# Six of ten token tiles transposed by VectorE in 32-blocks and put in place through DRAM, in place of TensorE's transposes

## The chip, the cores and the metric

One core of a Trainium2 chip runs the whole kernel. The core has a matrix engine (TensorE, PE in the profile), a vector engine (VectorE, DVE), a scalar engine (ScalarE, ACT), GpSimd (POOL) and SyncE (SP), whose queue issues nearly all DMAs here; 16 DMA engines carry them out. The metric is device time in microseconds, the median of a few runs. Lower is better.

## The reference

One encoder layer (depth 1, so the convolution mixer and no mLSTM) on 1024 prompt tokens and 256 sample tokens, model width 1024, in float32:

```python
h = rms_norm(x, norms[i, 0])
mix = short_conv_mixer(h, conv_w_in[j], conv_w[j], conv_w_out[j])
x = x + rms_norm(mix, norms[i, 1])
h = rms_norm(x, norms[i, 2])
x = x + rms_norm(swiglu(h, ffn_w_in[i], ffn_w_out[i]), norms[i, 3])
```

`short_conv_mixer` is a product to three times the width, a gated convolution over three tokens, and a product back to the width (`conv_w_out`); `swiglu` is a product to 2 x 2816 columns, `silu(gate) * up`, and a product back.

## The kernel before

Every float32 product is done as three products of high and low parts (`TERMS`), and the products over prompt tokens by a Strassen scheme over quarters of the operands (a11, a12, a21, a22 and their sums s1 to s4). The 1280 tokens are ten tiles of 128 (`i` = 0 to 9; 8 and 9 are the sample tokens). The stages, in order:

1. The first product and the convolution, features on partitions. The gated result, in high and low parts, goes to DRAM as `zd`.
2. The second product, `mm2`, one token tile at a time in the order 0, 4, 1, 5, 2, 6, 3, 7, 8, 9 (`ORDER2`), tokens on partitions. `load_z` brings a tile's operand from `zd` to `zs`; `mm2(i)` makes 48 products of 512 columns into two PSUM banks `mx`. Then `after_mm2(i)` runs six steps: ScalarE squares `mx` (sums `n1`), a factor is made by VectorE and GpSimd, VectorE makes `x1` = scaled `mx` plus the input tile `xt` and SP stores it to DRAM (`x1d`), ScalarE squares `x1` (sums `n2`), another factor, and VectorE writes the normalised tile `ht`.
3. The FFN needs the tokens on the free axis. `transposes(i)` turns `ht` in eight 128x128 pieces on TensorE into two PSUM banks `tr`; ScalarE and VectorE copy them into the quarters `ar` (`ar[0, 0]` is a11, `ar[1, 1]` is a22; the second index is the half of the tokens). In stage 2 the transposes of a tile stand inside the `mm2` of the tile two places later.
4. The FFN's two products, and the last norm.

`early_sums` splits the high and low parts of a slice of a11 and makes the slice's Strassen sums in place, as soon as the two token tiles of that slice are in `ar`. The first FFN weights `F0` are loaded and split in the same stretch (`wgf0`, `wuf0`, then at `n == 6` `wt24f0`, `wt13f0`). The last of these take buffer places that `zs` of a finished tile leaves (`wt13f0` takes that of `zs6`).

What sets the order: stage 2 is left to a scheduler, which writes one instruction list for each engine; an engine runs its list strictly in order, and so does SP with its DMAs. The entry to the FFN (`entry`, with tiles 8 and 9) is written out by hand. Buffers are places that are handed on: `get` takes the place longest free, `put` gives one back, and whoever takes a place waits for all that still use it. The kind "a" has three places, for `xt` and `x1`, kind "s" two, for `ht`. PSUM banks are taken in turn, eight of them (`new_ps`), but in `entry` by fixed numbers: the product of tile 8 in 4 and 5, that of 9 in 2 and 3, the transposes of tile 3 in 6 and 7, those of tile 7 in 0 and 1.

Of the kernel before, what the change touches and what calls it, by code (L numbers as in the profile page):

```python
# [8 lines left out]
F32 = mybir.dt.float32  # L9
# [5 lines left out]
P = 128  # L15
D = 1024
KD = D // P
# [19 lines left out]
def encoder_kernel(ctx: ExitStack, tc: tile.TileContext, xT, x, g0T, gB, cwT, w1, w2, w3, w4, out_p, out_s):  # L37
    nc = tc.nc
# [6 lines left out]
    dram = ctx.enter_context(tc.tile_pool(name="dram", bufs=1, space=bass.MemoryType.DRAM))  # L45
# [12 lines left out]
    def get(name, shape, dt=F32, kind="b"):  # L58
        if kind == "as":
            kind = "s" if free["s"] else "a"  # L60
        tag = free[kind].pop(0)
        t = mem.tile([P, *shape], dt, tag=tag, name=name)
        held[id(t)] = (t, tag)
        return t

    def put(*tiles):
        for t in tiles:
            tag = held.pop(id(t))[1]
            free[tag[0]].append(tag)
# [13 lines left out]


    zd = dram.tile([2, len(UNITS), P, 2, KD, P], F32, tag="zd", name="zd")
    x1d = dram.tile([NT, P, D], F32, tag="x1d", name="x1d")
    actd = dram.tile([len(UNITS), KP, P, 14 * P], F32, tag="actd", name="actd")

# [16 lines left out]
    def copy(out, a):  # L105
        nc.scalar.activation(out, a, AF.Copy)  # L106
# [3 lines left out]
    def new_ps(name, bank=None):  # L110

        if bank is None:
            bank = turn[0] % 8
            turn[0] += 1
        return ps.tile([P, 512], F32, tag=f"bank{bank}", name=name)
# [55 lines left out]
    def load(u, left=True, right=True):  # L171
        if u is None:
            return
        if u not in raw:
            raw[u] = get(f"wr{uname(u)}_", [4, 512])
        if u[0] == "p":
            tiles = [w1[u[1] * KD + 2 * u[2] + h] for h in (0, 1)]
        else:
            tiles = [w3[h * KF + u[1]] for h in (0, 1)]
        tiles = [t.rearrange("p (b c) -> p b c", b=2) for t in tiles]  # L180
        if left:
            nc.sync.dma_start(raw[u][:, 0:4:3], tiles[0])
        if right:
            nc.sync.dma_start(raw[u][:, 1:3], tiles[1])

    def make(u, what):

        if u is None:
            return
        rw = raw[u]  # L190
        if what == "sums":
            sub(rw[:, 0], rw[:, 1], rw[:, 0])
            sub(rw[:, 1], rw[:, 2], rw[:, 1])
            sub(rw[:, 2], rw[:, 0], rw[:, 2])
            add(rw[:, 3], rw[:, 3], rw[:, 2])
            return
        blocks = {"g": slice(0, 4, 3), "u": slice(1, 3), "t13": slice(0, 2), "t24": slice(2, 4)}[what]
        t = wb[what, u] = get(f"w{what}{uname(u)}_", [2, 2, 512], F32R)
        split(t[:, 0], t[:, 1], rw[:, blocks])
        sums_made[u] = sums_made.get(u, 0) + what.startswith("t")  # L200
        if sums_made[u] == 2:
            put(raw.pop(u))
# [577 lines left out]
    def load_z(i, k0=0, k1=KD):  # L780
        if i not in zs:
            zs[i] = get(f"zs{i}", [2, KD, P], F32R)
        src = zd[i // 4, i % 4] if i < 8 else zd[i - 8, 4]
        nc.sync.dma_start(f32(zs[i][:, :, k0:k1]), src[:, :, k0:k1])

    ORDER2 = [i for uu in UNITS for i in uu]
# [30 lines left out]
    ar = {(kh, c): get(f"ar{kh}{c}", [KH, 512]) for kh in (0, 1) for c in (0, 1)}  # L817
    hts, mx = {}, {}

    def transposes(i, banks=(None, None)):  # L820
        for q in range(2):
            o = new_ps(f"tr{i}_{q}", banks[q])
            for k in range(4):
                nc.tensor.transpose(
                    o[:, k * P : (k + 1) * P], hts[i][:, (4 * q + k) * P : (4 * q + k + 1) * P], ident
                )
            ov = o.rearrange("p (k t) -> p k t", k=4)
            if i < 8:
                t0 = i % 4 * P
                dst = ar[q, i // 4][:, :, t0 : t0 + P]  # L830
                if q:
                    nc.vector.tensor_copy(dst, ov)
                else:
                    copy(dst, ov)
            else:
                t0 = (i - 8) * P
                copy(hs[0][:, 4 * q : 4 * q + 4, t0 : t0 + P], ov)
                left.append((i, q, ov))
        put(hts.pop(i))

    left = []

    def take_left():
# [6 lines left out]
    def mm2(*tiles, ks=range(KD)):  # L850
        for i in tiles:
            if i not in mx:
                mx[i] = [new_ps(f"mx{i}_{h}", MX_BANKS.get((i, h))) for h in range(2)]
        for k in ks:
            for i in tiles:
                for j, (w, part) in enumerate(TERMS):
                    for h in range(2):
                        nc.tensor.matmul(  # L858
                            mx[i][h], zs[i][:, part, k], w2t[k][:, w, h * H : (h + 1) * H],
                            start=k == 0 and j == 0, stop=k == KD - 1 and j == 2,  # L860
                        )
# [38 lines left out]
    def after_mm2(i):  # L900
        for step in (norm_squares, norm_factor, norm_residual, norm_squares2, norm_factor2, norm_end):
            step(i)
# [3 lines left out]
    def load_xt(i):  # L906
        xts[i] = get(f"xt{i}", [D], kind="a")
        nc.sync.dma_start(xts[i], x[i])
# [4 lines left out]
    def early_sums(t):  # L913

        a, b, d = (q[:, :, t] for q in (a11, a21, a22))
        split(*(q[:, :, t] for q in cb["a11"]), a)
        add(b, b, d)
        sub(a, a, b)
        add(s3[:, :, t], d, a)
# [6 lines left out]
    for n, i in enumerate(ORDER2[:8]):  # L926
        if n == 0:
            mm2(i, ORDER2[1])
        elif n > 1:
            early = KD - 2 if n < 4 else 4  # L930
            mm2(i, ks=range(early))
            transposes(ORDER2[n - 2])
            mm2(i, ks=range(early, KD))
            if n == 4:
                cb["a11"] = [get(f"a11{p}", [KH, 512], F32R) for p in "hl"]
                s3 = get("s3", [KH, 512])
                early_sums(slice(0, P))
            if n == 6:
                early_sums(slice(P, 2 * P))
        after_mm2(i)  # L940
        if n:
            load_z(ORDER2[n + 1])
            load_xt(ORDER2[n + 1])
        if n == 4:
            load(F0)
            for what in ("g", "u", "sums"):
                make(F0, what)
        if n == 6:
            for what in ("t24", "t13"):
                make(F0, what)  # L950
# [691 lines left out]
```

## Time and profile before

| | |
|---|---|
| median of 3 runs | 1252.47 us (1251.35 to 1254.31) |
| the profiled execution | 1250.58 us |
| its span, first to last instruction | 1248.7 us |
| granted TensorE clock, mean | 0.998 |
| TensorE busy | 1236.0 us (99%) |
| VectorE / ScalarE / GpSimd busy | 835.0 / 463.9 / 25.6 us |
| DMA | 207.37 MB, 166 GB/s on average |

A row of a timeline reads: start, length (both us), engine, line, operation, out<-in, shapes, how many, and in brackets how long the engine stood idle before it and what ended that. SPq is SP's queue issuing a DMA. A row of the chain reads: start, length, engine, tile and line, how many. A row of waits reads: who waited for whom, total us, times, longest. A row of windows reads: the stretch, its length, busy time and instructions of PE, weight loads, VectorE, ScalarE and GpSimd, the granted clock, the share of the DMA engines, GB/s. A row of DMA issues reads: out<-in, queue, how many, KB each, median us from issue to landing; of DMA queues: packets, MB, the share of 16 engines' time. Numbers in names are left out there, so `tr`, `ar`, `zs` stand for all tiles; stage 2 runs from about 311 to 429 us.

### The profile page before, as it was taken

The numbers are of one execution on the slowest core, as the hardware profiler recorded it, in microseconds if no ns is written. First come the engines' busy times: TensorE is split into PE (matmuls) and PEld (weight loads), VectorE is DVE, ScalarE is ACT, GpSimd is POOL, SyncE is SP. The second block draws the span as 40 slices with busy tenths as digits, with TensorE's granted clock in tenths as the row PEclk, the third lists the DMA queues.
The fourth block names the chain that finished last, engine by engine and source line by source line (L and its number), as shares of the span: only waits on it lengthen the run. The fifth ranks groups of instructions, "written<-read, shape, count | busy, mean of one in ns | idle before, by whom it ended". The sixth has DMA issues, their size and how long they took to land.

```text
span 1248.7 us, 15941 instructions
## 1 busy us (share of the span) xinstructions
PE 1236.0 (99%) x6239; PEld 1052.2 (84%) x6239; DVE 835.0 (67%) x1157; ACT 463.9 (37%) x695; POOL 25.6 (2%) x49
## 2 busy tenths in 40 slices
PE   9999999999999999999999999999999999999997
PEld 7888888888888888888888888888888888888886
DVE  6986856657376787475466564755657479869566
ACT  8643333234233554343343343443434342102011
POOL 0000000000010100000000000000000000000000
PEclk9999999999999999999999999999999999999999
DMA  8323041416854215254262452542626798766894
GB/s 307 123 85 110 34 152 35 118 51 221 303 184 168 85 61 172 89 178 127 92 194 88 150 160 89 182 129 87 194 95 205 259 315 303 275 209 220 287 329 178
DMA packets 186123, 207.37 MB, mean 166 GB/s; under 512 B 8000, under 2 KB 146368, under 8 KB 185024
## 3 DMA queue, kind: packets, MB, share of 16 engines
q1 hardware_dynamic: 185616, 205.83, 49.1%
q8 instruction: 49, 0.80, 0.3%
q10 hardware_dynamic: 432, 0.53, 0.1%
q14 instruction: 26, 0.21, 0.1%
HBM read 134.89 MB, written 71.43 MB: 165 GB/s over the span
## 4 chain that ended last, share of the span: by engine, by line
PE 91%; DMA 3%; DVE 3%; ACT 2%; issue 1%; SPq 0%; POOL 0%; POOLq 0%; DVEq 0%; ACTq 0%
PE xo L1441 12%; PE mx L858 6%; PE zo L1441 6%; PE yo L1441 3%; DMA wrf__3033<-w 1%; PE xp__1068 L213 1%; PE xf__3503 L213 1%; PE xp__901 L213 1%; PE xf__7645 L213 1%; PE xf__7466 L213 1%; PE xf__7253 L213 1%; PE xf__7079 L213 1%; PE xf__6866 L213 1%; PE xf__6692 L213 1%; PE xf__6479 L213 1%; PE xf__6305 L213 1%
## 5 line engine op out<-in xcount | busy, mean ns | idle before, releaser
L858 PE MATMUL mx<-w2s,zs 128*128 128x512 f32 x480 | 111.1, 391 | 0.0
L858 PEld LDWEIGHTS mx<-w2s,zs 128*128 128x128 f32 x480 | 89.5, 188 | 18.3
L106 ACT ACTIVATE st<-act 128x640 fp32r<-128x640 f32 x77 | 56.8, 737 | 93.8 <-DMA actd<-st 62.9
L97 DVE TENSOR_TENSOR st<-act,st 128x640 fp32r<-128x640 f32 x77 | 63.2, 821 | 21.4 <-ACT st L106 20.9
L100 DVE TENSOR_TENSOR y<-y,xo 128x512 f32<-128x512 f32 x85 | 58.2, 685 | 27.4 <-PE xo L1441 27.1
L1441 PE MATMUL xo<-w4t,us 128*128 128x512 f32 x273 | 68.9, 389 | 0.0
L1441 PEld LDWEIGHTS xo<-w4t,us 128*128 128x128 f32 x273 | 51.2, 188 | 10.7
L1441 PE MATMUL xo<-w4t,ut 128*128 128x512 f32 x222 | 55.5, 389 | 0.0
L106 ACT ACTIVATE w4t<-w4r 128x1024 fp32r<-128x1024 f32 (+1 forms) x23 | 23.5, 1023 | 72.1 <-DVE w4r L97 58.4
L1441 PEld LDWEIGHTS xo<-w4t,ut 128*128 128x128 f32 x222 | 41.7, 188 | 8.7
L100 DVE TENSOR_TENSOR y<-y,zo 128x512 f32<-128x512 f32 x45 | 30.8, 685 | 17.3 <-PE zo L1441 17.0
L1441 PE MATMUL xo<-w4b,ut 128*128 128x512 f32 x165 | 41.6, 390 | 0.0
L1441 PE MATMUL zo<-w4t,ut 128*128 128x512 f32 x165 | 41.5, 389 | 0.0
L1441 PE MATMUL zo<-w4b,ut 128*128 128x512 f32 x165 | 41.5, 389 | 0.0
L1473 ACT ACTIVATE junk<-y 128x1024 f32<-128x1024 f32 (+1 forms) x12 | 11.0, 919 | 73.7 <-DVE y L100 72.4
L1441 PEld LDWEIGHTS xo<-w4b,ut 128*128 128x128 f32 x165 | 31.0, 188 | 6.6
L1441 PEld LDWEIGHTS zo<-w4t,ut 128*128 128x128 f32 x165 | 31.0, 188 | 6.5
L1441 PEld LDWEIGHTS zo<-w4b,ut 128*128 128x128 f32 x165 | 31.0, 188 | 6.4
L430 DVE SCALAR_TENSOR_TENSOR row<-u,cw,row 128x1024 f32<-128x1024 f32 (+1 forms) x32 | 27.7, 880 | 3.7 <-ACT row L428 3.5
L106 ACT ACTIVATE w4b<-w4r 128x512 fp32r<-128x512 f32 (+1 forms) x22 | 18.1, 838 | 30.7 <-DMA us<-actd 12.5
L1441 PE MATMUL yo<-w4b,us 128*128 128x512 f32 x114 | 28.9, 389 | 0.0
L97 DVE TENSOR_TENSOR w4t<-w4r,w4t 128x1024 fp32r<-128x1024 f32 (+1 forms) x23 | 26.9, 1173 | 0.8 <-ACT w4t L106 0.8
(2115 smaller groups left out, 3346.2 us busy)
## 6 DMA issues: line engine op xcount, KB each, us to landing
actd<-st SPq DMA_DIRECT2D x154, 320.0 KB, 2.8
ut<-actd SPq DMA_DIRECT2D x20, 1024.0 KB, 6.1
us<-actd SPq DMA_DIRECT2D x62, 256.0 KB, 5.0
ut<-actd SPq DMA_DIRECT2D x16, 768.0 KB, 8.2
zd<-zst SPq DMA_DIRECT2D x32, 320.0 KB, 3.2
zs<-zd SPq DMA_DIRECT2D x8, 1024.0 KB, 6.0
w4r<-w SPq DMA_DIRECT2D x11, 512.0 KB, 4.0
w4r<-w SPq DMA_DIRECT2D x22, 256.0 KB, 5.5
```

Of the source, the lines that this page charges most:

```text
L97: nc.vector.tensor_tensor(out=out, in0=a, in1=b, op=ALU.subtract)
L100: return nc.vector.tensor_tensor(out=out, in0=a, in1=b, op=ALU.add)
L106: nc.scalar.activation(out, a, AF.Copy)
L213: nc.tensor.matmul(out[:, :n], stat(w, k), mov(part, k), start=first and k == 0 and j == 0, stop=last and k == KH - 1 and j == 2, skip_gro ...
L430: nc.vector.scalar_tensor_tensor(out=out, in0=src, scalar=cw[:, j, dd : dd + 1], in1=out, op0=ALU.mult, op1=ALU.add)
L858: nc.tensor.matmul(mx[i][h], zs[i][:, part, k], w2t[k][:, w, h * H : (h + 1) * H], start=k == 0 and j == 0, stop=k == KD - 1 and j == 2,)
L1441: nc.tensor.matmul(acc, stat[n, c, j][:, ap], w[wp], start=starts and jn == 0 and m == 0, stop=jn == len(grp) - 1 and m == 2, skip_group_c ...
L1473: nc.scalar.activation(junk, src, AF.Square, accum_out=acc[:, col : col + 1])
```

## The change

Tiles 0, 4, 1, 5, 2 and 6 are no longer turned by TensorE. `turn_out(i, n)`, called after `after_mm2(i)`, has VectorE transpose `ht` in blocks of 32 tokens by 32 features into `vt` (kind "a"), picking features four apart so that each block row is a run of 32 tokens, and stores it by four DMAs to a DRAM buffer `hd`, each in 1024 pieces of 128 bytes. `turn_in`, one step later, loads the tile from `hd` into the two quarters `ar` in pieces of 512 bytes. Tiles 3, 7, 8 and 9 are turned as before.

```diff
+    hd = dram.tile([6, P, KD, P], F32, tag="hd", name="hd")
...
+    def turn_out(i, n):
+
+        h = hts.pop(i)
+        v = get(f"vt{i}", [4, KD, 32], kind="a")
+        nc.vector.transpose(v.rearrange("p q k t -> p k q t"), h.rearrange("p (k j q) -> p k q j", j=32, q=4))
+        put(h)
+        dst = hd[n].rearrange("(j q) k t -> j (q k) t", q=4)
+        for g in range(4):
+            nc.sync.dma_start(
+                dst[:, :, 32 * g : 32 * g + 32], v[32 * g : 32 * g + 32].rearrange("j q k t -> j (q k) t")
+            )
+        put(v)
+
+    def turn_in(i, n):
+        for q in range(2):
+            nc.sync.dma_start(ar[q, i // 4][:, :, i % 4 * P : i % 4 * P + P], hd[n, :, 4 * q : 4 * q + 4])
...
         elif n > 1:
-            early = KD - 2 if n < 4 else 4
-            mm2(i, ks=range(early))
-            transposes(ORDER2[n - 2])
-            mm2(i, ks=range(early, KD))
+            mm2(i)
...
+        if n < 6:
+            turn_out(i, n)
+        if 0 < n < 7:
+            turn_in(ORDER2[n - 1], n - 1)
```

The scheduler orders stage 2 anew. Three places of the new lists follow; a digit behind a name is the token tile, and the number after it only tells buffers apart.

SP's queue. Before, from the store of the first tile's `x1` on (`x1d`), the loads of `zs` for tiles 3 and 7 stand between the stores and input loads of tiles 0 to 2:

```order
L884 DMA x1d_107<-x1_0_2703 128x1024
L908 DMA xt1_2747<-x 128x1024
L784 DMA zs3_3134<-zd_106 128x2048
L884 DMA x1d_107<-x1_4_2729 128x1024
L908 DMA xt5_2839<-x 128x1024
L884 DMA x1d_107<-x1_1_2821 128x1024
L908 DMA xt2_2931<-x 128x1024
L784 DMA zs7_3231<-zd_106 128x2048
```

Now the same two loads, and that of tile 8, stand here:

```order
L902 DMA x1d_108<-x1_6_3109 128x1024
L785 DMA zs3_3125<-zd_106 128x2048
L926 DMA xt3_3127<-x 128x1024
L850 DMA hd_107<-vt6_3129 1024x1x32 x4
L857 DMA ar00_2584<-hd_107 128x4x128
L857 DMA ar10_2586<-hd_107 128x4x128
L785 DMA zs7_3218<-zd_106 128x2048
L926 DMA xt7_3220<-x 128x1024
L902 DMA x1d_108<-x1_3_3202 128x1024
L857 DMA ar01_2585<-hd_107 128x4x128
L857 DMA ar11_2587<-hd_107 128x4x128
L785 DMA zs8_3306<-zd_106 128x2048
```

The load of `zs3` has moved from behind the first `x1` store to behind the sixth (tiles 0, 4, 1, 5, 2, 6), that of `zs7` from behind the third to behind the stores of tile 6's `vt`.

ScalarE, before, from tile 5's second squares (`j_n2_5`) on:

```order
L132 ACTIVATE j_n2_5_0_2919,n2_5_2918<-x1_5_2913 128x512
L132 ACTIVATE j_n2_5_1_2921,n2_5_2918<-x1_5_2913 128x512
L106 ACTIVATE ar00_2583<-tr1_0_2959 128x4x128
L93 ACTIVATE a11h_2995<-ar00_2583 128x4x128
L132 ACTIVATE j_n1_2_0_3004,n1_2_3003<-mx2_0_2933 128x512
L132 ACTIVATE j_n1_2_1_3006,n1_2_3003<-mx2_1_2934 128x512
L93 ACTIVATE wt24f0__3235<-wrf0__3033 128x1024
L132 ACTIVATE j_n2_2_0_3019,n2_2_3018<-x1_2_3013 128x512
L132 ACTIVATE j_n2_2_1_3021,n2_2_3018<-x1_2_3013 128x512
L106 ACTIVATE ar01_2584<-tr5_0_3072 128x4x128
L132 ACTIVATE j_n1_6_0_3109,n1_6_3108<-mx6_0_3046 128x512
L132 ACTIVATE j_n1_6_1_3111,n1_6_3108<-mx6_1_3047 128x512
```

Before, `wt13f0` follows these. Now:

```order
L94 ACTIVATE wt24f0__3224<-wrf0__3036 128x1024
L94 ACTIVATE a11h_2990<-ar00_2584 128x4x128
L94 ACTIVATE wt13f0__3227<-wrf0__3036 128x1024
L133 ACTIVATE j_n2_5_0_2918,n2_5_2917<-x1_5_2912 128x512
L133 ACTIVATE j_n2_5_1_2920,n2_5_2917<-x1_5_2912 128x512
L133 ACTIVATE j_n1_2_0_2999,n1_2_2998<-mx2_0_2940 128x512
L133 ACTIVATE j_n1_2_1_3001,n1_2_2998<-mx2_1_2941 128x512
L133 ACTIVATE j_n2_2_0_3014,n2_2_3013<-x1_2_3008 128x512
L133 ACTIVATE j_n2_2_1_3016,n2_2_3013<-x1_2_3008 128x512
L133 ACTIVATE j_n1_6_0_3100,n1_6_3099<-mx6_0_3049 128x512
L133 ACTIVATE j_n1_6_1_3102,n1_6_3099<-mx6_1_3050 128x512
```

`wt24f0` and `wt13f0` have moved ahead of tile 5's second squares; the copies out of `tr` are gone.

VectorE, before, from tile 5's `ht` to tile 2's `x1`:

```order
L895 SCALAR_TENSOR_TENSOR ht5_2927<-x1_5_2913,n2_5t_2923,gb_2580 128x1024
L832 COPY ar10_2585<-tr1_1_2965 128x4x128
L94 TENSOR_TENSOR a11l_2996<-ar00_2583,a11h_2995 128x4x128
L141 SCALAR_TENSOR_TENSOR n1_2t_3008<-n1_2_3003,rq_105 128x1
L122 TENSOR_SCALAR n1_2t_3008<-n1_2t_3008 128x1
L879 SCALAR_TENSOR_TENSOR x1_2_3013<-mx2_0_2933,n1_2t_3008,gb_2580 128x512
L879 SCALAR_TENSOR_TENSOR x1_2_3013<-mx2_1_2934,n1_2t_3008,gb_2580 128x512
```

Now:

```order
L913 SCALAR_TENSOR_TENSOR ht5_2926<-x1_5_2912,n2_5t_2922,gb_2581 128x1024
L142 SCALAR_TENSOR_TENSOR n1_2t_3003<-n1_2_2998,rq_105 128x1
L846 STREAM_TRANSPOSE vt5_2932<-ht5_2926 128x8x4x32
L123 TENSOR_SCALAR n1_2t_3003<-n1_2t_3003 128x1
L101 TENSOR_TENSOR ar01_2585<-ar01_2585,ar11_2587 128x4x128
L98 TENSOR_TENSOR ar00_2584<-ar00_2584,ar01_2585 128x4x128
L101 TENSOR_TENSOR s3_2992<-ar11_2587,ar00_2584 128x4x128
L897 SCALAR_TENSOR_TENSOR x1_2_3008<-mx2_0_2940,n1_2t_3003,gb_2581 128x512
L897 SCALAR_TENSOR_TENSOR x1_2_3008<-mx2_1_2941,n1_2t_3003,gb_2581 128x512
```

The transpose and the three early sums of a slice have come in between tile 5's `ht` and tile 2's `x1`; the copy out of `tr` has gone.

## The prediction, made before the changed kernel was run

> **What bounds the kernel now.** I read the page first, for the share of each engine and the chain that ended last, then the chain in order of time around the stage that is changed, then the waits of TensorE there, then the queues of the other engines in the same stretch.
>
> ```profile
> PE 1236.0 (99%) x6239; PEld 1052.2 (84%) x6239; DVE 835.0 (67%) x1157; ACT 463.9 (37%) x695; POOL 25.6 (2%) x49
> ...
> PE 91%; DMA 3%; DVE 3%; ACT 2%; issue 1%; SPq 0%; POOL 0%; POOLq 0%; DVEq 0%; ACTq 0%
> ```
>
> TensorE is busy 99% of the span and makes 91% of the chain, so it sets the end, and what the transposes cost on it is a real cost. The chain in order of time, in the stage of the second product (mx) and the transposes (tr):
>
> ```profile
> 342.27 1.06 PE tr L824 x8
> 343.34 10.92 PE mx L858 x48
> 354.26 0.87 PE tr L824 x8
> 355.13 8.18 PE mx L858 x36
> 363.31 0.87 PE tr L824 x8
> 364.19 10.90 PE mx L858 x48
> ```
>
> A token tile is 48 products in 10.9 us; its eight transposes take 0.87 us between them. TensorE waited only once here, for the first tile to be transposed:
>
> ```profile
> PE tr L824 <- DVE n_4t L141: 0.8, 1, 0.8
> ```
>
> So TensorE ran from tile to tile without a stop, because the input of each product, zs, came early. In the timeline of the SP queue the load of tile 3's zs is issued at 346.12, some 35 us ahead of the product that reads it (tile 6's product, the one ahead of it, ends where ScalarE's next squares begin, at 381.24 below):
>
> ```profile
> 346.12 0.32 SPq L784 DMA_DIRECT2D zs<-zd x1
> 347.99 0.32 SPq L884 DMA_DIRECT2D x1d<-x x1
> ...
> 356.09 0.32 SPq L884 DMA_DIRECT2D x1d<-x x1
> ...
> 398.34 0.32 SPq L884 DMA_DIRECT2D x1d<-x x1
> ```
>
> **What the change takes away.** Six of the ten groups of eight transposes leave TensorE: 6 x 0.87 = 5.2 us, all on the path. With tile 0's group goes the one wait, 0.8 us. Together 6.0 us less. Twelve copies out of PSUM go too (half on ScalarE, half on VectorE); neither engine is on the path in these stretches, so I count them as nothing.
>
> **What it adds on the queues.** Per tile: one VectorE transpose, four stores of 1024 pieces of 128 bytes, two loads. These 36 transfers all stand in SP's queue, and in the new order the load of zs for tile 3 stands behind the store of tile 6's x1 (the order rows above show it). A queue passes nothing. The x1 of tile 6 exists only once tile 6's product is done and normalised, and the next product on TensorE is tile 3's, which needs that zs. So a transfer that was 35 us early becomes one that starts after the work before it has ended: TensorE must stop. The same holds, more mildly, for the zs of tile 7 (behind tile 6's stores) and of tile 8 (behind tile 3's x1).
>
> How long is the stop? Let T be the end of tile 6's product. In the new order of ScalarE the high part of the weights wt13f0 stands ahead of tile 5's second squares. Its place is the one that zs6 leaves, free at T. In the order before, it stood behind tile 6's first squares, where T had passed anyway:
>
> ```profile
> 356.10 0.63 ACT L132 ACTIVATE j_n<-x 128x512 f32<-128x512 f32 x1 [5.62 <-DVE x L100]
> ...
> 381.24 0.60 ACT L132 ACTIVATE j_n<-mx 128x512 f32<-128x512 f32 x1 [3.00 <-PE mx L858]
> ...
> 382.40 1.06 ACT L93 ACTIVATE wt13f__3238<-wrf__3033 128x1024 fp32r<-128x1024 f32 x1
> ...
> 393.02 0.60 ACT L132 ACTIVATE j_n<-mx 128x512 f32<-128x512 f32 x1 [2.89 <-PE mx L858]
> ```
>
> So from T on, what is left of tile 5, all of tile 2 and the first half of tile 6 must run in a row on ScalarE, VectorE and GpSimd before SP gets to zs of tile 3. VectorE's timeline has every step of it once, for tile 1:
>
> ```profile
> 352.32 0.15 DVE L122 TENSOR_SCALAR n_1t<-n_1t 128x1 f32<-128x1 f32 x1
> 353.39 1.41 DVE L879 SCALAR_TENSOR_TENSOR x<-mx,n_1t,gb 128x512 f32<-128x512 f32 x2 [0.92 <-POOL n_1t L146]
> 354.84 1.23 DVE L100 TENSOR_TENSOR x<-x,xt 128x1024 f32<-128x1024 f32 x1
> 357.47 0.16 DVE L100 TENSOR_TENSOR n_1t<-n 128x1 f32<-128x1 f32 x1 [1.41 <-ACT j_n L132]
> 357.66 0.15 DVE L122 TENSOR_SCALAR n_1t<-n_1t 128x1 f32<-128x1 f32 x1
> 358.48 1.28 DVE L895 SCALAR_TENSOR_TENSOR ht<-x,n_1t,gb 128x1024 f32<-128x1024 f32 x1 [0.66 <-POOL n_1t L123]
> 359.68 0.68 DVE L832 COPY ar<-tr 128x512 f32<-128x512 f32 x1
> 360.47 0.69 DVE L100 TENSOR_TENSOR ar<-ar,ar 128x512 f32<-128x512 f32 x1
> 361.20 0.69 DVE L97 TENSOR_TENSOR ar<-ar,ar 128x512 f32<-128x512 f32 x1
> 361.92 0.69 DVE L100 TENSOR_TENSOR s<-ar,ar 128x512 f32<-128x512 f32 x1
> 362.53 0.21 DVE L141 SCALAR_TENSOR_TENSOR n_5t<-n,rq 128x1 f32<-128x1 f32 x1
> 362.78 0.15 DVE L122 TENSOR_SCALAR n_5t<-n_5t 128x1 f32<-128x1 f32 x1
> ```
>
> Steps, start to start, so that the hops between engines are in them: squares to sum 357.47 - 356.10 = 1.37; sum to ht 358.48 - 357.47 = 1.01; ht 359.68 - 358.48 = 1.20; next tile's factor 0.25; the three sums 362.53 - 360.47 = 2.06; x1, from its first half to the squares that read it, 356.10 - 353.39 = 2.71; factor to x1, 1.07. The VectorE transpose has no row. Nearest is ht, the same 1024 numbers per partition, 1.20; at half rate it would be 2.4. It does one pass over the same bytes, so I take 1.2. The Trainium skill, "VectorE: DVE Perf Modes", section "The three transpose paths", gives 311 ns for 128x128 in bf16, eight of them 2.5 us as an estimate; by it this sum would be 2.6 us longer, and no row here shows it.
>
> - Tile 5's rest: 1.06 + 1.37 + 1.01 + 1.20 + 0.25 + 1.2 = 6.1.
> - The three early sums of the second slice: 2.1.
> - Tile 2: 2.71 + 1.37 + 1.01 + 1.20 + 0.25 + 1.2 = 7.7.
> - Tile 6: 1.07 + 2.71 = 3.8, then the issue of its x1 store, 0.3.
> - zs of tile 3, issue to landing, with a share of 1.2 for the megabyte (two loads, one store) issued just ahead of it: at 403 GB/s that is 2.6 us, half of it past.
>
> ```profile
> zs<-zd SPq DMA_DIRECT2D x2, 1024.0 KB, 5.8
> xt<-x SPq DMA_DIRECT2D x1, 512.0 KB, 3.5
> ...
> DMA packets 1004, 5.24 MB, mean 403 GB/s; under 512 B 99, under 2 KB 112, under 8 KB 492
> ```
>
> 5.8 + 1.2 = 7.0. The stop: 6.1 + 2.1 + 7.7 + 3.8 + 0.3 + 7.0 = 27.0 us. The loads of xt (3.5) fall inside the 7.7 of a tile and stay hidden.
>
> After it, zs of tile 8 is issued behind tile 3's x1: 398.34 - 393.02 = 5.3 after tile 3's product, plus two loads of ar and its own 5.8, some 12.5 against the 10.9 of tile 7's product. The banks change as well: with twelve banks fewer taken in turn, tile 7's product now lies in banks 6 and 7, which the transposes of tile 3 ask for right after tile 8's first six products; they wait for tile 7's x1. The two waits overlap; I take 3 us for both (2 to 4).
>
> A stop of 27 us is long enough for the clock. At the end of the program TensorE stops at 1240.8 and the granted clock is halved in the next stretch; at the start the first products ran slow until 5.9, 4.4 us after the first one:
>
> ```profile
> 1240.00:1245.00 5.00, 0.79 (x4) 0.33 (x2) 4.25 (x9) 1.15 (x4) 1.45 (x2) 1.00 0.22 83
> 1245.00:1249.00 4.00, 0.00 (x0) 0.00 (x0) 0.54 (x1) 0.00 (x0) 0.00 (x0) 0.50 0.43 161
> ```
> ```profile
> 1.49 3.78 PE L451 MATMUL warmup<-idle 128*128 128x512 f32 x4 [1.49 <-DVE idle L448]
> 4.82 0.87 PE L213 MATMUL c__157<-a11h,wc 128*128 128x512 f32 x1
> ...
> 5.92 0.40 PE L213 MATMUL c__157<-a11h,wc 128*128 128x512 f32 x1
> ```
>
> 4.4 us at half rate lose 2 us (bounds 0 and 2.2).
>
> **The price of a short store.** Not in the trace. Around it: 1312 packets, nearly all of 512 bytes, took 26.6% of 16 engines for 8 us, 26 ns each; 115 of 32 bytes took 3.2% of 16 engines for 2 us, 9 ns each.
>
> ```profile
> q1 hardware_dynamic: 1312, 0.66, 26.6%
> ...
> q10 hardware_dynamic: 115, 0.00, 3.2%
> ```
>
> The lower row is a load; 128 bytes is nearer to it in size, but what is priced is a store, so I take 18, the middle: 256 packets per engine and tile, 4.6 us. At that price a tile's stores pass while VectorE works on, and they are in the sum only by the 1.2 above.
>
> **Sum.** -6.0 + 27.0 + 3 + 2 = +26.0 on the profiled execution's 1250.58: 1276.6. That execution was 1.9 under the median of 1252.47, so the median comes to 1278.5, say **1279**. Behind this stage the order of the engines is as it was, so the loss is carried to the end.
>
> **Rivals.**
> A. The stores become the bound. Each tile's xt goes into the place that the tile before left to its four stores, so it waits for them to land: a tile's period is at least 256 packets at their price plus 3.5 for xt. That passes TensorE's 10.9 from 29 ns on. The Trainium skill, "DMA: Bandwidth & Descriptors", section "Specifications", speaks for this one: under 512 bytes the engine reads, modifies and writes. As a mechanism of this kernel: if a short store costs two passes of 26 ns, 52 ns, a tile is 13.3 + 3.5 = 17 us. Tile 4's x1 is made just before its store at 347.99, say at 347; four periods later, at 415, tile 6's; zs of tile 3 then runs behind tile 2's stores, 13.3 + 5.8, and lands at 434, where TensorE was ready at 377 (381.2 less the wait of 0.8 and the four transposes before it, 3.5): a stop of 57, and 7 for tile 7. -6 + 57 + 7 + 2 = +60: 1312. Against it: the 9 ns of the smallest packets.
> B. Only the floor of the stop: if ScalarE and VectorE kept pace with TensorE, T to tile 6's x1 is 5.3, plus 0.3 and 5.8: 11.4. -6 + 11.4 + 3 + 2 = +10: 1263. Against it: ScalarE's order.
> C. Faster: the loads of zs stay hidden, TensorE never stops, and only the 6.0 counts: 1246. It decides where zs of tile 3 is issued more than 5.8 us before T; that needs a queue that lets a load pass a waiting store, of which nothing in the trace speaks.
>
> **Chances.** The forecast 0.68, A 0.20, B 0.08, C 0.03, no change 0.01. The range from 1266 to 1313 holds the forecast with its bounds (a transpose at half rate adds 2.4, prices from 9 to 28 ns take or add some 3, short landings take 2) and A up to 52 ns; it leaves out B, C and dearer stores. No change means within 0.2%, 2.5 us, about what a measurement of this kernel can tell. Slower 0.96, same 0.01, faster 0.03.
>
> **What would show it.** After: 48 transposes less and no wait ahead of the first; one idle of TensorE of 25 to 30 us ahead of tile 3's product, released by the DMA of zs; a clock under 1.00 just behind it; ScalarE idle ahead of wt13f until tile 6's product ends; zs of tile 3 issued right behind the sixth x1 store; a wait of 1 to 4 us at tile 8. A is right if SP waits for stores of hd ahead of each xt; B if ScalarE's squares follow each product at once. I am wrong if the zs load lands before T, or if short stores cost over 30 ns.

## The result, and the profile after

The changed kernel takes 1280.39 us (median, 1279.87 to 1281.4), the kernel before 1251.91 in the same comparison: a ratio of 1.0238, 95% interval 1.0226 to 1.025, or 28.5 us more. The profiled execution took 1280.07 us with a span of 1278.3, against 1250.58 and 1248.7 before: 29.6 us more span to explain.

From the page: the busy times, the granted clock in slices, and the group of the second product (busy, mean ns, idle before it and what ended the idle):

```profile
PE 1234.2 (97%) x6191; PEld 1050.8 (82%) x6191; DVE 843.2 (66%) x1157; ACT 461.0 (36%) x689; POOL 27.0 (2%) x49
...
PEclk9999999999995999999999999999999999999999
...
L876 PE MATMUL mx<-w2s,zs 128*128 128x512 f32 x480 | 113.4, 398 | 33.3 <-DMA zs<-zd 29.1
```

TensorE has 48 instructions less, as the change says. Its busy time fell only from 1236.0 to 1234.2, and one slice has half the clock. The second product now has 33.3 us of idle time ahead of it; before, TensorE had waited once in this stage, 0.8. The list of TensorE's waits in the stage, each with its sum, count and longest:

```profile
PE mx L876 <- DMA zs<-zd: 29.1, 1, 29.1
PE mx L876 <- DVE x L897: 4.2, 1, 4.2
```

So two stops. TensorE's timeline gives their places, in brackets the idle time before the row and what ended it:

```profile
405.35 24.27 PE L876 MATMUL mx<-w2s,zs 128*128 128x512 f32 x96 [29.12 <-DMA zs<-zd]
433.84 2.74 PE L876 MATMUL mx<-w2s,zs 128*128 128x512 f32 x6 [4.22 <-DVE x L897]
```

The first is the stop ahead of tile 3's product, from 376.23 to 405.35; the products of tiles 3 and 7 behind it take 24.27 us for their 96 instructions, where two tiles take 21.8 at full speed. The second stop comes ahead of tile 8's product.

The second stop is also a wait for a load, though the profile names VectorE. A row names the event that came last before the engine went on, and two events lie together here:

```profile
426.20 0.69 SPq L785 DMA_DIRECT2D zs<-zd  x1
...
433.05 1.41 DVE L897 SCALAR_TENSOR_TENSOR x<-mx,n_7t,gb 128x512 f32<-128x512 f32 x2 [0.92 <-POOL n_7t L147]
```

The first row is the load of tile 8's zs; in the trace its last piece lands at 433.71. The second is tile 7's x1, whose first half ends at 433.8. By the program tile 8's first products need that zs and the banks 4 and 5, which tile 3's x1 had left at 422.65. They do not need tile 7's x1: the product for the other half of the columns begins at 434.24, before the second half of that x1 ends (434.46). So this stop, too, ends with a zs that came late.

What the other engines did in the first stop stands in their timelines: ScalarE,

```profile
376.27 1.06 ACT L94 ACTIVATE wt13f__3227<-wrf__3036 128x1024 fp32r<-128x1024 f32 x1 [9.30 <-PE mx L876]
```

then VectorE,

```profile
380.92 1.98 DVE L846 STREAM_TRANSPOSE vt<-ht 128x1024 f32<-128x1024 f32 x1
...
391.64 1.96 DVE L846 STREAM_TRANSPOSE vt<-ht 128x1024 f32<-128x1024 f32 x1
...
396.38 1.23 DVE L101 TENSOR_TENSOR x<-x,xt 128x1024 f32<-128x1024 f32 x1
```

then the SP queue, first the four stores of tile 5's transpose; zs of tile 3 is the row at 398.33, right behind the x1 store of tile 6 at 397.78:

```profile
382.93 2.97 SPq L850 DMA_DIRECT2D hd<-vt  x4
...
397.78 0.45 SPq L902 DMA_DIRECT2D x1d<-x  x1
398.33 0.38 SPq L785 DMA_DIRECT2D zs<-zd  x1
```

ScalarE had stood idle for 9.3 us until T, the end of tile 6's product (376.2). VectorE worked its way through tiles 5, 2 and 6, and SP got to zs 22.1 us after T. The load then took 7.0 to land. Sums over stretches show the price behind the stops (columns: length, busy time of PE, PEld, DVE, ACT and POOL, then the granted clock, the DMA share and GB/s):

```profile
380.00:402.00 22.00, 0.00 (x0) 0.00 (x0) 16.55 (x24) 4.45 (x13) 3.40 (x6) 0.50 0.70 178
406.00:410.00 4.00, 4.00 (x11) 3.17 (x10) 0.00 (x0) 0.00 (x0) 0.00 (x0) 0.50 0.92 168
410.00:414.00 4.00, 4.00 (x18) 3.28 (x18) 0.00 (x0) 0.00 (x0) 0.00 (x0) 0.98 0.96 313
434.00:436.00 2.00, 2.00 (x6) 1.53 (x6) 1.68 (x2) 0.00 (x0) 0.00 (x0) 0.51 1.03 433
```

The clock is at 0.50 during the stop and stays there until about 410, 4.7 us after TensorE started again. At 434 it is at 0.51 once more, behind the short stop.

### The profile page after: what moved, and what is told of

The parts are those of the page before. It is cut to its first block, busy times and chain, and to the rows that moved or that the text cites. A ratio compares the mean times of both kernels' runs of the same rounds, so it can differ in the third digit from the quotient of the medians.

```text
span 1278.3 us, 15899 instructions
## 1 busy us (share of the span) xinstructions
PE 1234.2 (97%) x6191; PEld 1050.8 (82%) x6191; DVE 843.2 (66%) x1157; ACT 461.0 (36%) x689; POOL 27.0 (2%) x49
## 4 chain that ended last, share of the span: by engine, by line
PE 62%; DVE 0%; issue 0%; POOLq 0%; DVEq 0%
PE xo L1460 12%; PE zo L1460 6%; PE yo L1460 3%; PE xf__7622 L214 1%; PE xf__7443 L214 1%; PE xf__7230 L214 1%; PE xf__7056 L214 1%; PE xf__6843 L214 1%; PE xf__6669 L214 1%; PE xf__6456 L214 1%; PE xf__6282 L214 1%; PE xf__6069 L214 1%; PE xf__5895 L214 1%; PE xf__5682 L214 1%; PE xf__5508 L214 1%; PE xf__5295 L214 1%
## 5 line engine op out<-in xcount | busy, mean ns | idle before, releaser
L876 PE MATMUL mx<-w2s,zs 128*128 128x512 f32 x480 | 113.4, 398 | 33.3 <-DMA zs<-zd 29.1
L876 PEld LDWEIGHTS mx<-w2s,zs 128*128 128x128 f32 x480 | 92.1, 193 | 53.3 <-DVE ar L98 29.5
L98 DVE TENSOR_TENSOR st<-act,st 128x640 fp32r<-128x640 f32 x77 | 63.2, 821 | 19.1 <-ACT st L107 18.6
L133 ACT ACTIVATE j_n<-mx 128x512 f32<-128x512 f32 x20 | 11.6, 586 | 51.1 <-PE mx L876 51.1
L107 ACT ACTIVATE w4b<-w4r 128x512 fp32r<-128x512 f32 (+1 forms) x22 | 18.1, 838 | 30.1 <-PE zo L1460 12.5
```

The source lines that it names most:

```text
L98: nc.vector.tensor_tensor(out=out, in0=a, in1=b, op=ALU.subtract)
L133: nc.scalar.activation(junk, src, AF.Square, accum_out=acc[:, h : h + 1])
L876: nc.tensor.matmul(mx[i][h], zs[i][:, part, k], w2t[k][:, w, h * H : (h + 1) * H], start=k == 0 and j == 0, stop=k == KD - 1 and j == 2,)
```

## The experiments

Three theories, mine and two against it. **Queue** (the prediction): zs of tile 3 stands behind the x1 store of tile 6 in SP's queue, and that x1 comes at the end of a chain of steps over ScalarE, VectorE and GpSimd. **Stores** (rival A): the 24576 packets of 128 bytes cost the time. **VectorE**: its transposes themselves cost it, wherever the loads stand.

### The zs loads from another queue

```diff
-        nc.sync.dma_start(f32(zs[i][:, :, k0:k1]), src[:, :, k0:k1])
+        q = nc.scalar if i in (3, 7, 8, 9) else nc.sync
+        q.dma_start(f32(zs[i][:, :, k0:k1]), src[:, :, k0:k1])
```

> One edit on the changed kernel: the loads of zs for tiles 3, 7, 8 and 9 are issued from ScalarE's queue, all else stays. If SP's queue is the cause (zs of tile 3 stands behind tile 6's x1 store), the stop of 29 us ahead of tile 3's product goes. VectorE's chain stays as late as it was (x1 of tile 6 came 22 us after that tile's product), so TensorE meets it one or two tiles later: stops of together 14 to 18 us ahead of tile 8's product and tile 3's transposes, released by VectorE; 1258 to 1267. If the short stores are the cause, it stays at 1277 to 1282, with zs landing late from the other queue too. If VectorE's transposes as such are the cause, the whole wait only moves: 1275 to 1280.

1264.5 us, ratio 1.0115 (1.0101 to 1.0129). ScalarE's queue and TensorE's waits:

```profile
343.98 0.33 ACTq L786 DMA_DIRECT2D zs<-zd  x1
```

```profile
PE mx L877 <- DVE x L898: 14.1, 1, 14.1
PE tr L826 <- DVE x L898: 4.5, 1, 4.5
```

The stop ahead of tile 3 is gone, as zs is issued 32 us ahead of T. About half of the loss stays: VectorE's chain, still late, now holds TensorE at tile 8 (14.1) and at tile 3's transposes (4.5). So the queue place was the wait that ended last, and a late chain stood right behind it, with stops of 18.6 us in all. The first expectation holds in its time, with stops a little above its 14 to 18; the packets were the same, so Stores falls as the cause of the 29 us.

### The places of two weights

The chain's first step, by the prediction, is that wt13f0 waits on ScalarE for the place that zs of tile 6 leaves at T. Here the places of both weights are taken two tiles earlier, and only used later:

```diff
-        t = wb[what, u] = get(f"w{what}{uname(u)}_", [2, 2, 512], F32R)
+        if (what, u) not in wb:
+            wb[what, u] = get(f"w{what}{uname(u)}_", [2, 2, 512], F32R)
+        t = wb[what, u]
...
+        if n == 4:
+            for what in ("t24", "t13"):
+                wb[what, F0] = get(f"w{what}{uname(F0)}_", [2, 2, 512], F32R)
         if n == 6:
             for what in ("t24", "t13"):
                 make(F0, what)
```

> One edit on the changed kernel: the places of the weights wt24f0 and wt13f0 are taken two tiles earlier, so that their high parts on ScalarE no longer need the place that zs of tile 6 leaves at T. If the prediction's first step is right (wt13f0 waits for T in front of tile 5's second squares, and tile 5's rest, 6.1 us, is therefore behind T), ScalarE does not stop for T there, zs of tile 3 is issued some 6 us sooner, and the stop ahead of tile 3's product falls from 29 to 22 to 24: 1272 to 1276. If ScalarE's wait is not on the path (VectorE was late anyway), the stop stays at 28 to 30 and the time at 1278 to 1282.

1275.86 us, ratio 1.0206 (1.0192 to 1.022). The waits, then VectorE's additions of xt to x1 (tiles 1, 5, 2 and 6), then SP:

```profile
PE mx L878 <- DMA zs<-zd: 30.0, 2, 25.6
```

```profile
362.34 1.22 DVE L101 TENSOR_TENSOR x<-x,xt 128x1024 f32<-128x1024 f32 x1 [1.77 <-DMA xt<-x]
...
372.13 1.23 DVE L101 TENSOR_TENSOR x<-x,xt 128x1024 f32<-128x1024 f32 x1
...
382.56 1.23 DVE L101 TENSOR_TENSOR x<-x,xt 128x1024 f32<-128x1024 f32 x1
...
392.35 1.23 DVE L101 TENSOR_TENSOR x<-x,xt 128x1024 f32<-128x1024 f32 x1
```

```profile
394.30 0.38 SPq L787 DMA_DIRECT2D zs<-zd  x1
```

The two stops are 25.6 and 4.4; the time is in the expected range, the first stop longer than its 22 to 24. zs of tile 3 is issued 4.0 us sooner (394.30 against 398.33), so ScalarE's wait was on the path. That it is not 6 sooner doesn't make the wait shorter than forecast. The edit also changed the scheduler's order, and here VectorE adds xt to tile 5's x1 at 372.13, 2.5 us later than in the changed kernel, whose rows for this step are

```profile
369.67 1.22 DVE L101 TENSOR_TENSOR x<-x,xt 128x1024 f32<-128x1024 f32 x1
...
377.23 0.61 ACT L133 ACTIVATE j_n<-x 128x512 f32<-128x512 f32 x1
```

There tile 5's x1 was ready at 370.9, and its squares began at 377.23, behind wt13f: a wait of 6.3 us.

The four rows of this run show why a late VectorE doesn't recover: from tile to tile they are 9.8, 10.4 and 9.8 us apart, and a product takes 10.9. It gains about 1 us a tile at most, so a chain that is most of a tile late stays late.

### The rotation of PSUM banks

```diff
             mm2(i)
+            turn[0] += 2
```

> One edit on the changed kernel: each tile's product skips two PSUM banks, so the rotation of banks is as it was before the change and tile 7's product no longer lies in banks 6 and 7. If those banks made the wait of 4.2 us ahead of tile 8 (released by VectorE's x), a wait for x is gone there and one for the DMA of zs of 2 to 4 us stands in its place. Since each product now takes the banks of the tile two before, small waits for x1 may come ahead of tiles 2 and 6. The stop ahead of tile 3 is then shorter by as much. In all 1276 to 1281. If the banks cost time of their own, 1274 or less.

1286.21 us, ratio 1.0286 (1.0267 to 1.0305): slower still, and outside what I expected. TensorE's timeline, and one stretch:

```profile
358.18 12.78 PE L876 MATMUL mx<-w2s,zs 128*128 128x512 f32 x48 [3.50 <-DVE x L897]
374.63 0.51 PE L876 MATMUL mx<-w2s,zs 128*128 128x512 f32 x1 [3.67 <-DVE x L897]
...
413.00 23.86 PE L876 MATMUL mx<-w2s,zs 128*128 128x512 f32 x96 [25.16 <-DMA zs<-zd]
441.11 2.90 PE L876 MATMUL mx<-w2s,zs 128*128 128x512 f32 x6 [4.25 <-DMA zs<-zd]
```

```profile
360.00:362.00 2.00, 2.00 (x6) 1.57 (x5) 0.49 (x1) 0.00 (x0) 0.00 (x0) 0.50 1.13 270
```

Ahead of tile 8 the same stop stands, 4.25, now named for zs: the banks had not made it, so other banks could not take it away. The new waits for x1 ahead of tiles 2 and 6 (3.5 and 3.7) came as said, but I took them for small. Each also slowed the clock: behind the first it was 0.50 from 360 to 362, and the 48 products took 12.8 us and not 10.9; those of tile 6 took 13.2, from 374.63 to 387.84.

### The stage in an order written out by hand

The loop over the tiles becomes one order for all engines (the core of it; the rest spreads the first unit's weights over the tiles, sets PSUM banks, copies both halves of the remaining transposes on ScalarE, and makes ht of tile 9 one step earlier):

```python
        for n in range(2, 8):
            i = O[n]
            mm2(i)
            norm_squares(i)
            if n < 7:
                load_z(O[n + 3])
            load_xt(O[n + 1])
            norm_factor(i)
            ...
            norm_residual(i)
            norm_squares2(i)
            ...
            if n < 7:
                turn_out(O[n - 1], n - 1)
            norm_factor2(i)
            norm_end(i)
            ...
            if n < 7:
                turn_in(O[n - 2], n - 2)
```

> The changed kernel with the stage's order written out by hand: each zs load three tiles ahead and before any store in SP's queue, the DVE transpose of a tile placed into the next tile's wait for its squares, the weights of the first unit spread over the tiles, fixed PSUM banks. The same six tiles are transposed by VectorE with the same 24576 short packets. If the queue order is the cause, no stop of TensorE over 2 us is left in the stage and what remains is the work taken from TensorE, 5.2 to 6: 1245 to 1249. If the short stores are the cause: 1270 or more. If VectorE's time is the cause (12 us more of it in a stretch of 80 us): stops of a few us at the tiles' ends, 1251 to 1257.

Its control keeps the order and gives all ten tiles back to TensorE:

```diff
-            mm2(i)
+            early = KD - 2 if n < 4 else 4
+            mm2(i, ks=range(early))
+            transposes(O[n - 2], [MX_BANKS[O[n - 2], h] for h in range(2)])
+            mm2(i, ks=range(early, KD))
...
-            if n < 7:
-                turn_out(O[n - 1], n - 1)
...
-            if n < 7:
-                turn_in(O[n - 2], n - 2)
```

> The same hand order with all ten tiles transposed by TensorE, as before the change: the control for the order itself. If the order as such is worth nothing: 1250 to 1254, and the difference to the hand order with VectorE's transposes is their own worth, 5 to 7. If the order as such gains: below 1249.

1249.23 us, ratio 0.9988 (0.998 to 0.9997), for the six tiles; 1249.86, ratio 0.9997 (0.9988 to 1.0006), for the control. So the same transposes and the same packets that cost 28 us in one order cost nothing in another, and the order as such is worth nothing measurable. **VectorE** falls with that as the cause of the loss: its transposes don't cost it wherever the loads stand. But the gain is 0.6 us over the control and not 5, and where I expected no stop over 2 us one of 4.3 is left. The wait and two stretches of the six tiles' run:

```profile
PE tr L825 <- DVE ht L910: 4.3, 1, 4.3
```

```profile
365.00:398.00 33.00, 33.00 (x147) 27.36 (x146) 22.12 (x34) 7.71 (x22) 3.81 (x9) 1.00 0.95 261
...
404.00:406.00 2.00, 2.00 (x9) 1.95 (x10) 1.93 (x4) 0.00 (x0) 0.00 (x0) 0.50 0.96 274
```

A stop of 4.3 us and a slow stretch behind it took the gain. From 365 to 398 TensorE never stops and the DMA engines are 95% busy. From 342 to 398 they were 49% busy in the kernel before (first row; 52% in the control), and are 87% here (second):

```profile
342.00:398.00 56.00, 55.73 (x266) 46.67 (x267) 39.28 (x66) 19.10 (x50) 7.46 (x17) 1.00 0.49 171
```

```profile
342.00:398.00 56.00, 56.00 (x248) 46.39 (x248) 38.19 (x55) 13.75 (x39) 7.22 (x15) 1.00 0.87 233
```

The SP queue shows it from the other side, and VectorE's x1 behind it:

```profile
374.05 0.50 SPq L785 DMA_DIRECT2D zs<-zd  x1
375.26 0.34 SPq L923 DMA_DIRECT2D xt<-x  x1
375.65 0.74 SPq L899 DMA_DIRECT2D x1d<-x  x1
377.14 7.93 SPq L847 DMA_DIRECT2D hd<-vt  x4
```

```profile
352.12 1.41 DVE L894 SCALAR_TENSOR_TENSOR x<-mx,n_1t,gb 128x512 f32<-128x512 f32 x2 [4.36 <-DMA hd<-vt]
...
372.37 1.41 DVE L894 SCALAR_TENSOR_TENSOR x<-mx,n_2t,gb 128x512 f32<-128x512 f32 x2 [4.88 <-DMA x1d<-x]
```

Behind zs, xt and x1 (2 MB) the four stores of a tile hold SP for 7.9 us; in the changed kernel four took 3.0 (the row at 382.93) with none of these just ahead. VectorE's x1 waited 4.4 and 4.9 us for places that the stores and x1d had not yet left. From 365 to 414 SP issues almost without a gap, and the loads of zs stand 12.4 to 12.8 us apart (361.66, 374.05, 386.80, 399.64), where a product takes 10.9. That is the pace at which this order falls behind.

### The place in SP's queue alone

The control with one line moved: no VectorE transpose, no short store.

```diff
-            if n < 7:
+            if n < 7 and n != 3:
                 load_z(O[n + 3])
...
             norm_residual(i)
+            if n == 5:
+                load_z(O[6])
```

> The hand order with all ten tiles transposed by TensorE, and one thing of the change put back: the load of zs for tile 3 stands behind tile 6's x1 store in SP's queue. No VectorE transpose and no short store is in it. If the queue place alone makes the stop: from tile 6's product to its x1 5.3 us, issue 0.3, landing 5.8, so a stop of 11 to 12 ahead of tile 3's product and some 2 for the slow clock behind it: 11 to 15 us over the same order without the move (1249.9). If the loss needs the transposes or the short packets: within 2 us of it.

1264.4 us, ratio 1.0104 (1.009 to 1.0119), 14.5 over the control.

```profile
393.58 8.45 PE L873 MATMUL mx<-w2s,zs 128*128 128x512 f32 x24 [11.78 <-DMA zs<-zd]
```

The stop is 11.8, against 11.4 worked out from the rows of before, and the slow clock behind it adds to it. This is the floor that rival B described, seen alone: with a prompt chain the queue place costs 14.5 us. The change costs 28.5 although it also takes 6 from TensorE, so some 20 us come from the chain being late, which roughly agrees with the 18.6 of stops that stayed when zs came from ScalarE's queue.

### Four tiles, a later place, and every store twice

Tiles 2 and 6 go back to TensorE:

```diff
-            mm2(i)
+            if n < 6:
+                mm2(i)
+            else:
+                mm2(i, ks=range(4))
+                transposes(O[n - 2], [MX_BANKS[O[n - 2], h] for h in range(2)])
+                mm2(i, ks=range(4, KD))
...
-            if n < 7:
+            if n < 5:
                 turn_out(O[n - 1], n - 1)
...
-            if n < 7:
+            if n < 6:
                 turn_in(O[n - 2], n - 2)
...
```

> The hand order with four tiles transposed by VectorE in place of six (tiles 2 and 6 go back to TensorE). If the stop of 4.3 us ahead of tile 3's transposes came from the DMA engines (near 90% busy in that stretch, SP held 8 us by four stores), it goes with the two last tiles' short packets, and what is left is 4 x 0.87 + 0.8 = 4.3 us less on TensorE: 3 to 5 us under before, 1245 to 1247. If VectorE's or ScalarE's order makes the stop: 1247 to 1250, with a stop of 2 to 4 us left there.

1247.9 us, ratio 0.9981 (0.9971 to 0.999).

```profile
PE tr L825 <- DVE ht L910: 1.7, 1, 1.7
```

The stop falls from 4.3 to 1.7, and the time lies in the second expected range, with a stop below its 2 to 4. Four tiles are also 4 us less on VectorE, so this alone doesn't tell DMA time from VectorE's. Next, six tiles, with TensorE's transposes of tiles 3 and 7 further on in the products of tiles 8 and 9 (tile 7's by the like edit):

```diff
-        mm2(8, ks=range(1))
+        mm2(8, ks=range(5))
         transposes(ORDER2[6], (6, 7))
```

> The hand order with six tiles, but TensorE's transposes of tiles 3 and 7 stand four and three products' steps later (5.4 and 4.1 us) in the products of tiles 8 and 9. If the chain behind tile 3 is only late by 4 to 5 us, the stop ahead of those transposes and its slow clock go: 1243 to 1246. If the chain stays late, the wait turns up again at the first products of the next stage (released by VectorE's hsl or ScalarE's weights): 1246 to 1249.

1250.04 us, ratio 0.9995 (0.9984 to 1.0005).

```profile
PE xf__3478 L214 <- ACT c__3605 L107: 3.5, 1, 3.5
PE tr L825 <- DVE ht L910: 2.3, 2, 1.4
```

The wait only moved: 3.5 us turned up at the next stage's first products, the second branch of what I expected, and at 1250.04 a little above its range. Last, six tiles with every store twice:

```diff
-        for g in range(4):
+        for g in (0, 1, 2, 3, 0, 1, 2, 3):
```

> The hand order with six tiles, each of the 24 short stores issued twice (the same bytes to the same place): 24576 packets of 128 bytes more. If DMA time bounds the stage in this order: 4096 packets per tile at 12.5 ns over 16 engines are 3.2 us more per tile on engines that are about 90% busy, so some 2 to 3 us a tile come out as stops of TensorE, 12 to 20 us over the single stores. If short stores are hidden behind the products: within 2 us of the single stores. If a short store costs two passes of 26 ns: 40 us and more.

1273.14 us, ratio 1.0175 (1.016 to 1.019).

```profile
PE tr L825 <- DVE ht L910: 9.7, 3, 7.8
PE mx L873 <- DMA zs<-zd: 9.0, 3, 5.1
PE xf__3502 L214 <- ACT c__3629 L107: 3.5, 1, 3.5
```

This leaves VectorE's work as it is and costs 23.9 us over the single stores, above the 12 to 20 that I expected: 24576 packets at 12.5 ns over 16 engines are 19.2 us of DMA time, and stops of 22.2 us replace the 4.3. So with doubled stores the transfers bound the stage. Whether it is the engines or SP's issuing that does it, the run doesn't say. The engines are 91% busy from 365 to 398, less than the 95% of the single stores, and SP's queue is held longer:

```profile
371.85 11.75 SPq L847 DMA_DIRECT2D hd<-vt  x8
```

The loads of zs now stand 15.7 to 16.8 us apart. One estimate speaks for the engines: eight stores held SP for 6.8 us where little was ahead of them (the first eight, at 346.35), and 2 MB at the 403 GB/s of the prediction's row are 5.2 us; together 12.0, about the 11.75. By this estimate the queue is held because the engines are behind. That the stop of 4.3 with single stores came from the transfers too is what VectorE's waits for places say; the runs don't separate it further from VectorE's own 12 us.

Then four tiles again, with tile 3's transposes two steps later (`range(3)` in place of `range(1)` in that line).

> The hand order with four tiles by VectorE, and TensorE's transposes of tile 3 two products' steps (2.7 us) later in the product of tile 8. If the 1.7 us that they waited is only lateness of that one chain, the stop goes and nothing takes its place: 1245 to 1247. If the chain behind stays late, a wait of 1 to 2 us at the next transposes or at the first products of the next stage: 1247 to 1249.

1247.43 us, ratio 0.998 (0.9971 to 0.9989) to the kernel before, 1249.86 in that comparison. No stop is left in the stage; 1.6 us stay at the next one, where the kernel before waits 0.8, so the second expectation holds:

```profile
PE sgf__3782 L214 <- DVE hsl L98: 1.6, 1, 1.6
```

This is faster than both kernels: 2.4 us (0.2%) under the kernel before, where four groups and the first wait come to 4.3. A high DMA share alone makes no stop: from 342 to 398 this run has 87% as well.

## Why the prediction was right, step by step

**The order of things held.** TensorE stopped ahead of tile 3's product, released by the DMA of zs, which was issued right behind the sixth x1 store; ScalarE idled ahead of wt13f until T. Each was named beforehand, and the moved load alone makes such a stop (11.8 for 11.4 worked out). What makes it 29.1 is the late chain behind T, which the prediction had step by step.

**The sum, term by term,** on the span:

| term | predicted | measured |
|---|---|---|
| taken from TensorE, with the first wait | -6.0 | 48 instructions less, wait gone |
| stop ahead of tile 3 | 27.0 | 29.1 |
| stop at tile 8 | 3 | 4.2 |
| slow clock behind the stops | 2 | 3.4 |
| sum | 26.0 | 29.6 |

The 3.4 is TensorE's busy time: 1236.0 - 5.2 = 1230.8 was to be expected, 1234.2 it was. The measured terms with the -6.0 come to 30.7; TensorE's idle time elsewhere fell by the other 1.1, and where it fell is open. Of the 3.4, the products of tiles 3 and 7 lost 24.3 - 21.8 = 2.5 behind the first stop, for which I had 2; the rest belongs to the second stop, for which I had counted no slow clock.

**The stop was 2.1 too short by its chain** (22.1 to the issue of zs, where I had 20.0); the landing of 7.0 was right. The term mis-sized is the VectorE transpose: 1.98 us, 1.9 from start to start, where I took 1.2 from ht of the same size. Two lie in the chain: 1.4. The other 0.7 lies mainly in two small steps: tile 6's factor to x1 took 1.42 where I had 1.07, the issue of its x1 store 0.55 where I had 0.3. The trace has no such transpose before; my bound at half rate, 2.4, holds the measured value. The Trainium skill's figure ("VectorE: DVE Perf Modes", section "The three transpose paths"), 2.5 us as an estimate, was 0.5 too dear where mine was 0.8 too cheap.

**Tile 5's rest** was 6.6 of the chain where I had 6.1; the transpose is the difference. The reason held as well: tile 5's squares stood 6.3 us behind their ready x1. The run with earlier places won 4.0 of that, as its VectorE was 2.5 later.

**Tile 8.** Here half of the reasoning failed, and the size came near in part by luck. I counted on zs 12.5 us after tile 3's product and on a wait for banks behind it, and took 2 to 4 for both. The banks cost nothing: the transposes of tile 3, which need them, followed tile 8's six products without a stop. The whole 4.2 was zs, which landed 15.1 us after tile 3's product (418.6 to 433.7), 7.5 of it from its issue, for which I had taken 5.8. The runs with other banks and other places show 4.25 and 4.4 for the same stop.

**The short store** cost less than the 18 ns that I took. One tile's four stores, with nothing else in the queue:

```profile
q1 hardware_dynamic: 4160, 0.52, 55.4%
```

55.4% of 16 engines for 5.5 us over 4160 packets are 11.7 ns; over the run the mean of the packets of 128 bytes is 12.5. Rival A needed 29 ns, and a price of two passes (52 ns) shows in no run. The Trainium skill's rule for packets under 512 bytes ("DMA: Bandwidth & Descriptors", section "Specifications"), that the engine reads, modifies and writes, is not borne out as a doubled time here; whether it reads first, no run shows. Yet A's mechanism is real, one step away: with TensorE no longer stopped, the same stores bring the DMA engines to 95%, and twice as many set the pace, through the engines or through SP's queue. **Rival C**, 1246, named its condition, zs of tile 3 issued more than 5.8 us before T. Met from ScalarE's queue, that was not enough (1264.5), since the chain behind was late too.

## What to carry to other kernels

Work taken off the bounding engine can be lost again in the order of a queue: ask of each load which store stands ahead of it, and what that store waits for. When one wait is taken away, look for the chain behind it: here the second was 19 us, and where both were gone the DMA engines were near full. When the profile names a releaser, ask whether the program needs it: a load can land at the same moment. Moving less (four tiles of six) kept more of the gain than moving all.

## What the runs showed of the hardware

- A VectorE transpose in blocks of 32 of 128x1024 f32 takes 1.96 to 2.04 us, 1.5 to 1.6 times the 1.28 of a plain operation on as many numbers (ht).
- A store in pieces of 128 bytes takes 11.7 to 13.1 ns a packet (the last is the mean in the order by hand), half of the 26 ns that the rows of before gave for packets of nearly all 512. That is half the bytes per time.
- SP's queue is itself held by the issue of many small packets: four stores of 1024 pieces took 3.0 us in one place and 7.9 with 2 MB just ahead.
- A short stop is enough for the clock. Behind 4.3 us (404 to 406 above) and behind 3.5 us it fell to 0.50, behind 1.7 us it did not; the first row is the six tiles with the later place, the second the four tiles:

```profile
445.00:447.00 2.00, 1.63 (x4) 1.34 (x5) 2.00 (x3) 1.81 (x4) 0.42 (x1) 0.50 0.00 0
```

```profile
404.00:406.00 2.00, 1.87 (x13) 1.70 (x14) 1.96 (x4) 0.39 (x2) 0.00 (x0) 1.00 0.31 125
```

The Trainium skill ("TensorE: Matmul & The Clock Gate", section "What's actually happening") says that one idle window of about 3.4 us halves the clock and one busy window restores it. The three stops agree with the first. For the second these runs show 3 to 6 us: full speed came back 3.0 us behind the restart in the six tiles' order (403.85 to about 406.9), and 5.8 where the load alone was moved. There TensorE restarts at 393.58, and a clock that is 0.50 until about 399.4 gives the 0.58 of this stretch:

```profile
396.00:400.00 4.00, 4.00 (x12) 3.10 (x11) 0.00 (x0) 0.00 (x0) 0.00 (x0) 0.58 0.03 10
```
